# Seven block products for 13 channel pairs of two feed-forward passes

## The chip, the core and the metric

The kernel runs on one core of one Trainium2 chip. The core has five instruction streams that run side by side and wait for one another by semaphores: TensorE (PE, with its weight loads listed apart as PEld), VectorE (DVE), ScalarE (ACT), GpSimd (POOL) and SyncE (SP), which issues the DMAs. On-chip memory is SBUF and, for matmul results, PSUM. The metric is the device time of one execution in microseconds (us).

## The reference

Two residual layers work on 1024 tokens of 1024 channels. Layer 0 mixes tokens by gating and sparse attention, layer 1 by a convolution module, and each layer ends in the same feed-forward block, which the change is about:

```
x <- LayerNorm(alpha * x + f(x))
f:  u = x @ w_up                      # 1024 channels -> 2 x 2816
    u = causal 3-tap depthwise conv(u) + bias
    f(x) = (gelu(u[:, :2816]) * u[:, 2816:]) @ w_down
```

All operands and results are float32.

## The kernel before

**Numbers.** A float32 operand is cut into a high part, which TensorE reads in its float32r format, and the rest (`split`, `wload`): ACT copies the high part, and POOL or DVE subtracts it from the operand. A product is then three matmuls into the same PSUM tile, high x rest, rest x high, high x high (`mm3`, L77 to L79). Weights come as tiles of 128 x 1024 float32, 512 KB: the DMA L69, the copy `wh` on ACT (L70) and two subtractions `wl` of 128 x 512 on POOL (L73).

**Feed-forward.** The tokens are two halves of 512 (h = 0, 1), so there are four passes `ffn(h, l)`: F00, F10, F01, F11, in this order. In a pass, `up(j)` treats channel pair j of 22: for each of the two column tiles of the pair it loads a weight tile, makes 8 x 3 matmuls of 512 columns into the PSUM tile `pu`, and takes the three taps on ACT (L678, L680) and DVE (L682, L683, which copies the last two columns at L685). The first tile goes through gelu (L688); POOL multiplies it by the second (L690) and splits the result into `ph` and `pl`. `down(gi)` multiplies a group of pairs by the down weights: groups of 8, 8 and 6 pairs (`KG`), each in two halves of the output columns with four PSUM tiles `pd`. At the end of a half, four adds on DVE bring `pd` into the residual Z (L396 for the first group, L398 after it).

**Order.** The Python generators yield at the ends of units; `go` and `mix` interleave them, and the tile framework's scheduler orders each engine's instructions from that, so that products of two tiles interleave. An engine works strictly in its order. A tile name has a fixed number of buffers, and a new tile waits for the last reader of the old one. The normalisation of Z and its transposition (`norm`) is mixed into the neighbouring passes: `norm(1, g0)` runs at the start of F00, and the output norm `final(0, g3)` at the start of F11.

Of the kernel before, what the change touches and what calls it, by code (L numbers as in the profile page):

```python
# [37 lines left out]
def trunk_kernel(ctx, tc, xt, wab, wv, w280, wst, sgub, sgulg, sgulb, pe_k, pe_v, w1k, w1v, w2k, w2v,  # L38
# [613 lines left out]
    hal = fp.tile([128, 44, 2], F32, name="halo")  # L652
    cor = fp.tile([128, 44, 2], F32, name="cor")

    def ffn(h, l, tail=None):
        xh, xl = XT[h]
        z = Z[h]
        cw = V[f"fw{l}"].rearrange("p (m k) -> p m k", k=3)
# [8 lines left out]
                nc.vector.tensor_tensor(cor[:, :, i], cor[:, :, i], V[cb], op=OP.add)  # L667
        prod = {}

        def up(j):  # L670
            acc = []
            for e in range(2):
                mt = 2 * j + e
                w = wload(wup[l, mt])
# [2 lines left out]
                a = tmp("acc")
                nc.scalar.activation(a[:, 2 * h:], p[:, 2 * h:], AF.Identity, scale=cw[:, mt, 2:3], bias=col(cb, mt))  # L678
                for i in range(2 * h):
                    nc.scalar.activation(a[:, i:i + 1], p[:, i:i + 1], AF.Identity, scale=cw[:, mt, 2:3],  # L680
                                         bias=cor[:, mt, i:i + 1])
                nc.vector.scalar_tensor_tensor(a[:, 1:], p[:, :511], cw[:, mt, 1:2], a[:, 1:], op0=OP.mult, op1=OP.add)  # L682
                nc.vector.scalar_tensor_tensor(a[:, 2:], p[:, :510], cw[:, mt, 0:1], a[:, 2:], op0=OP.mult, op1=OP.add)  # L683
                if h == 0:
                    nc.vector.tensor_copy(hal[:, mt, :], p[:, 510:512])  # L685
                acc.append(a)
# [3 lines left out]
            nc.gpsimd.tensor_tensor(acc[0], acc[0], acc[1], op=OP.mult)  # L690
            hi = fp.tile([128, 512], F32R, name="ph", tag="p", bufs=18)
            lo = fp.tile([128, 512], F32R, name="pl", tag="p", bufs=18)
            split(hi, lo, acc[0], nc.gpsimd)
            prod[j] = (hi, lo)
# [288 lines left out]
```

## Time and profile before

| what | value |
|---|---|
| median of 3 runs | 2340.69 us (2338.47 to 2340.94) |
| the profiled execution | 2340.53 us |
| its span in the trace | 2338.8 us |
| PE busy | 2293.3 us, 98% |
| POOL, DVE, ACT busy | 1391.8, 1176.0, 1008.9 us |
| up matmuls `pu` of 512 columns | 4320 rows in the trace |
| down matmuls `pd` | 656 rows in each of three lines |

The span leaves 1.7 us of the execution outside. A matmul's end is modelled and a matmul overlaps the next, so its cost is the time from one start to the next, not the duration in the row. The share of an engine over the span hides how the stages differ; the rows below are of single stages.

### The profile page before, as it was taken

To read this page: it belongs to the slowest core of one execution; us is meant where nothing else is said; L and a number is where in the kernel's file an instruction comes from. 1 tells how busy PE (TensorE), PEld (TensorE's weight loads), DVE (VectorE), ACT (ScalarE), POOL (GpSimd) and SP (SyncE) were. 2 spreads that over 40 slices of the span, in tenths; PEclk is the share of its full clock that TensorE was granted. 3 is DMA by queue.
4 is the path that set the end of the run, shared out by engine and by line. 5 is a ranking of instruction groups with operands and counts; after the bars stand their busy time and mean duration, and the time that the engine had idled before them with its cause. 6 is when DMAs were issued, how large, how long until landed. Compare 5 with 4: busy or idle time off the path is not lost.

```text
span 2338.8 us, 30101 instructions
## 1 busy us (share of the span) xinstructions
PE 2293.3 (98%) x10959; PEld 1914.5 (82%) x10959; DVE 1176.0 (50%) x2176; ACT 1008.9 (43%) x1786; POOL 1391.8 (60%) x1313
## 2 busy tenths in 40 slices
PE   9999899999999999999999999999999999999998
PEld 7888789887888888788888887788888887888886
DVE  2532898746322223579972325589961446212214
ACT  4133998733433323434344552434243633534441
POOL 4442777556665656655566575655565666666672
PEclk9999999999999999999999999999999999999999
DMA  6153121352332333233323233223323233323340
GB/s 227 35 144 98 50 64 54 105 194 92 99 99 90 99 95 95 84 97 99 99 91 99 90 108 101 85 95 100 99 91 99 89 110 135 96 95 99 99 135 37
DMA packets 82988, 232.23 MB, mean 99 GB/s; under 512 B 10079, under 2 KB 24039, under 8 KB 82840
## 3 DMA queue, kind: packets, MB, share of 16 engines
q1 hardware_dynamic: 82840, 230.30, 31.2%
q8 instruction: 87, 1.43, 0.3%
q14 instruction: 61, 0.50, 0.1%
HBM read 213.44 MB, written 8.43 MB: 95 GB/s over the span
## 4 chain that ended last, share of the span: by engine, by line
PE 93%; DVE 3%; ACT 1%; issue 1%; POOL 1%; DMA 0%; SPq 0%; DVEq 0%; ACTq 0%
PE pu L77 13%; PE pu L79 13%; PE pu L78 13%; PE pd L77 9%; PE pd L78 9%; PE pd L79 9%; PE pt L563 2%; PE pca L79 1%; PE pcg L79 1%; PE pcg L77 1%; PE pca L77 1%; PE pcg L78 1%; PE pca L78 1%; PE O L571 1%; PE O L570 1%
## 5 line engine op out<-in xcount | busy, mean ns | idle before, releaser
L73 POOL TENSOR_TENSOR wl<-wraw,wh 128x512 fp32r<-128x512 f32 x680 | 889.1, 1330 | 704.7 <-ACT wh L70 693.7
L77 PE MATMUL pu<-XTl,wh 128*128 128x512 f32 x1440 | 564.7, 392 | 5.9 <-DVE acc L683 3.7
L79 PE MATMUL pu<-XTh,wh 128*128 128x512 f32 x1440 | 563.6, 391 | 0.0
L78 PE MATMUL pu<-XTh,wl 128*128 128x512 f32 x1440 | 563.0, 391 | 0.0
L70 ACT ACTIVATE wh<-wraw 128x1024 fp32r<-128x1024 f32 x340 | 359.6, 1058 | 414.3 <-PE pd L79 352.9
L682 DVE SCALAR_TENSOR_TENSOR acc<-pu,vec,acc 128x511 f32<-128x511 f32 x176 | 131.8, 749 | 513.0 <-ACT acc L680 264.6
L77 PEld LDWEIGHTS pu<-XTl,wh 128*128 128x128 f32 x1440 | 271.8, 189 | 62.8 <-issue 4.1
L758 DVE SCALAR_TENSOR_TENSOR cacc<-ht,vec,cacc 128x512 f32<-128x512 f32 x464 | 318.5, 751 | 5.5 <-ACT cacc L754 3.9
L678 ACT ACTIVATE acc<-pu,vec 128x510 f32<-128x510 f32 (+1 forms) x176 | 137.3, 780 | 424.0 <-PE pu L79 423.8
L79 PEld LDWEIGHTS pu<-XTh,wh 128*128 128x128 f32 x1440 | 271.5, 189 | 56.8
L78 PEld LDWEIGHTS pu<-XTh,wl 128*128 128x128 f32 x1440 | 271.7, 189 | 56.2
L77 PE MATMUL pd<-wl,ph 128*128 128x512 f32 x656 | 259.1, 396 | 0.0
L78 PE MATMUL pd<-wh,pl 128*128 128x512 f32 x656 | 258.8, 394 | 0.0
L79 PE MATMUL pd<-wh,ph 128*128 128x512 f32 x656 | 256.7, 395 | 0.0
L79 PEld LDWEIGHTS pd<-wh,ph 128*128 128x128 f32 x656 | 123.5, 188 | 29.0
L78 PEld LDWEIGHTS pd<-wh,pl 128*128 128x128 f32 x656 | 123.7, 189 | 28.6
L77 PEld LDWEIGHTS pd<-wl,ph 128*128 128x128 f32 x656 | 123.6, 188 | 28.4
L398 DVE TENSOR_TENSOR Z<-Z,pd 128x512 f32<-128x512 f32 x64 | 43.5, 683 | 180.1 <-PE pd L79 180.0
L683 DVE SCALAR_TENSOR_TENSOR acc<-pu,vec,acc 128x510 f32<-128x510 f32 x176 | 131.5, 747 | 4.7
L690 POOL TENSOR_TENSOR acc<-acc 128x512 f32<-128x512 f32 x88 | 113.7, 1292 | 25.0 <-DVE acc L683 17.6
L396 DVE SCALAR_TENSOR_TENSOR Z<-Z,pd 128x512 f32<-128x512 f32 x64 | 43.6, 682 | 156.6 <-PE pd L79 156.6
L540 POOL TENSOR_SCALAR P<-P,sm 128x64 f32<-128x64 f32 (+6 forms) x192 | 107.4, 583 | 21.9 <-DVE sm L534 12.8
(252 smaller groups left out, 3790.4 us busy)
## 6 DMA issues: line engine op xcount, KB each, us to landing
wraw<-wup SPq DMA_DIRECT2D x176, 512.0 KB, 3.5
wraw<-wdn SPq DMA_DIRECT2D x82, 512.0 KB, 3.5
wraw<-cwin SPq DMA_DIRECT2D x32, 512.0 KB, 3.5
wraw<-wout SPq DMA_DIRECT2D x16, 512.0 KB, 4.3
wraw<-cwout SPq DMA_DIRECT2D x16, 512.0 KB, 3.5
wraw<-wab SPq DMA_DIRECT2D x14, 512.0 KB, 3.9
gb<-lns SPq DMA_DIRECT2D x12, 512.0 KB, 4.2
B<-fd SPq DMA_DIRECT2D x8, 512.0 KB, 3.4
```

Of the source, the lines that this page charges most:

```text
L70: nc.scalar.activation(wh[:, :n], raw[:, :n], AF.Copy)
L73: (leng or nc.gpsimd).tensor_tensor(wl[:, c], raw[:, c], wh[:, c].bitcast(F32), op=OP.subtract)
L77: nc.tensor.matmul(out_, ah, bl, start=first, stop=False)
L78: nc.tensor.matmul(out_, al, bh, start=False, stop=False)
L79: nc.tensor.matmul(out_, ah, bh, start=False, stop=last)
L540: nc.gpsimd.tensor_scalar(P[:, e, o:o + ln_], P[:, e, o:o + ln_], sm[:, e, i:i + 1], 0.0, op0=OP.mult, op1=OP.add)
L563: nc.tensor.transpose(pt[:, j, e * 128:(e + 1) * 128], P[:, e, o:o + kn], ident)
L678: nc.scalar.activation(a[:, 2 * h:], p[:, 2 * h:], AF.Identity, scale=cw[:, mt, 2:3], bias=col(cb, mt))
L682: nc.vector.scalar_tensor_tensor(a[:, 1:], p[:, :511], cw[:, mt, 1:2], a[:, 1:], op0=OP.mult, op1=OP.add)
L683: nc.vector.scalar_tensor_tensor(a[:, 2:], p[:, :510], cw[:, mt, 0:1], a[:, 2:], op0=OP.mult, op1=OP.add)
L690: nc.gpsimd.tensor_tensor(acc[0], acc[0], acc[1], op=OP.mult)
L758: nc.vector.scalar_tensor_tensor(c[0] if k else ht[:, :H], ht[:, k:k + H], dww[:, j, k:k + 1], c[0], op0=OP.mult, op1=OP.add)
```

## The change

Only F00 and F11 (`quick=True`) are changed, and in them pairs 3 to 15, 13 of 22 (`QUICK`). For these a pair's product is a 2 x 2 block product (two weight tiles, two halves of the 1024 input channels, two halves of the 512 tokens), and it is made from seven block products instead of eight, by sums of blocks. Each block product (`prod7`) is 4 x 3 matmuls of 256 columns. What goes in and comes out:

- `sums`, once a pass: sums of the four token blocks, kept split in the tiles TA and TB (M2 to M7 below read them or blocks of x itself).
- `prep(j)`, once a pair: two weight tiles `ra`, `rb`; four adds of 128 x 512 on DVE for the sums s1 to s4 of weight blocks, `ws` the tile of two of them; splits of both tiles and of the four sums.
- `up7(j)`: the seven products into the PSUM tiles `pa` and `pb`, and between them a copy on ACT and five adds of 128 x 256 on DVE. The taps, gelu, gating (`taps3`, `gated`: the lines of `up`, moved) are the same.
- `downs`: pairs 0 to 15 go down in four groups of four, cut into 16 units of 24 matmuls; one unit follows each pair from j = 4 on. A group's adds into Z come with its second unit of each half. The last six pairs stay as they were.
- `norm(1, g0)` moves from the start of F00 to after its pair 15, and between the four `final(0, g3)` steps F11 goes one step instead of two. The scale and offset tiles are loaded a second time (`affine`).

```diff
-    def mm3(out_, ah, al, bh, bl, first, last):
+    def mm3(out_, ah, al, bh, bl, first, last, more=False):
...
+        def sums():
+            ta, tb = A("xh", F32R, (128, 4, 4, 256), name="TA"), A("xl", F32R, (128, 4, 4, 256), name="TB")
...
+            for k in (0, 2):
+                u1, u2 = (fp.tile([128, 2, 2, 256], F32, name="ts", tag="nrm", bufs=2) for _ in range(2))
...
+                nc.gpsimd.tensor_tensor(b11, *f(k, 0), op=OP.add)
+                nc.vector.tensor_tensor(b12, *f(k, 256), op=OP.add)
+                nc.gpsimd.tensor_tensor(b21, *f(k + 4, 0), op=OP.add)
+                nc.vector.tensor_tensor(b22, *f(k + 4, 256), op=OP.add)
+                nc.vector.tensor_tensor(b22, b22, b12, op=OP.subtract)
+                nc.vector.tensor_tensor(b12, b12, b11, op=OP.subtract)
+                nc.vector.tensor_tensor(b11, b22, b11, op=OP.add)
+                nc.vector.tensor_tensor(b21, b21, b11, op=OP.subtract)
+                for n, t_, e in (("t2", b11, nc.vector), ("t1", b12, nc.gpsimd), ("t3", b22, nc.vector),
+                                 ("t4", b21, nc.gpsimd)):
+                    split(X7[n][0][:, k:k + 2], X7[n][1][:, k:k + 2], t_, e)
...
+        def prep(j):
+            ra, rb = W4(F32, name="wraw"), W4(F32, name="wraw")
+            nc.sync.dma_start(ra, wup[l, 2 * j])
+            nc.sync.dma_start(rb, wup[l, 2 * j + 1])
+            s_ = fp.tile([128, 1024], F32, name="ws", tag="nrm", bufs=2)
+            a, b = slice(0, 512), slice(512, 1024)
+            add = lambda o, x_, y_, op: nc.vector.tensor_tensor(o, x_, y_, op=op)
...
+            def pair(src):
+                h_, l_ = W4(F32R, name="wh", tag="wh"), W4(F32R, name="wl", tag="wl")
+                nc.scalar.activation(h_, src, AF.Copy)
+                for c in (a, b):
+                    nc.gpsimd.tensor_tensor(l_[:, c], src[:, c], h_[:, c].bitcast(F32), op=OP.subtract)
...
+            def one(src, eng):
+                h_, l_ = (fp.tile([128, 512], F32R, name=n, tag="ht", bufs=8) for n in ("sh", "sl"))
+                split(h_, l_, src, eng)
+                return h_, l_
+            add(s_[:, a], rb[:, a], rb[:, b], OP.add)
+            add(s_[:, b], s_[:, a], ra[:, a], OP.subtract)
+            w["11"], w["12"] = pair(ra)
+            w["s2"] = one(s_[:, b], nc.vector)
+            w["s1"] = one(s_[:, a], nc.vector)
+            yield w
+            add(rb[:, a], ra[:, a], rb[:, a], OP.subtract)
+            add(ra[:, b], ra[:, b], s_[:, b], OP.subtract)
+            w["s3"], w["22"] = pair(rb)
+            w["s4"] = one(ra[:, b], nc.gpsimd)
+            yield
...
+        def prod7(o, w, x_, first=True):
+            for k in range(4):
+                s_ = slice(k * 128, (k + 1) * 128)
+                mm3(o, w[0][:, s_], w[1][:, s_], x_[0][:, k, :], x_[1][:, k, :], first and k == 0, k == 3, not first)
...
+        def up7(j):
...
+            prod7(pa[:, c0], w["11"], X7["11"])
+            prod7(pb[:, c1], w["s2"], X7["t2"])
+            nc.scalar.activation(t_, pa[:, c0], AF.Copy)
+            add(t_, t_, pb[:, c1])
+            prod7(pa[:, c0], w["12"], X7["21"], False)
+            nxt = prep(j + 1) if j + 1 < QUICK[1] else None
+            prod7(pa[:, c1], w["s1"], X7["t1"])
+            add(v_, t_, pa[:, c1])
+            if nxt:
+                W7[j + 1] = next(nxt)
+            yield
+            prod7(pb[:, c0], w["s3"], X7["t3"])
+            add(pb[:, c1], v_, pb[:, c0])
+            prod7(pa[:, c1], w["s4"], X7["22"], False)
+            add(pa[:, c1], t_, pa[:, c1])
+            acc = [taps3(2 * j, pa)]
+            nc.scalar.activation(acc[0], acc[0], AF.Gelu_apprx_tanh)
+            prod7(pb[:, c0], w["22"], X7["t4"], False)
+            if nxt:
+                next(nxt)
+            add(pb[:, c0], t_, pb[:, c0])
+            acc.append(taps3(2 * j + 1, pb))
+            gated(j, acc)
+            yield
...
+            def downs():
+                units = [(a, dh, i) for a in range(0, 16, 4) for dh in range(2) for i in range(2)]
...
-    F00 = ffn(0, 0)
-    mix(norm(1, g0), F00, 1)
-    go(F00, 56)
+    F00 = ffn(0, 0, quick=True)
+    go(F00, 2 * QUICK[1])
+    g0 = affine(0)
+    mix(norm(1, g0), F00, 2)
+    go(F00, 4)
...
-    F11 = ffn(1, 1, final(1, g3))
+    F11 = ffn(1, 1, lambda tt: final(1, g3)(tt), quick=True)
```

What the order of instructions becomes is shown at three places of F00. On POOL before, one pair of the up part alternates a weight tile (two `wl`) with one operation on the products (`acc` the gating, `pl` the split):

```order
L73 TENSOR_TENSOR wl_7189<-wraw_7187,wh_7188 128x512 [waits DMAHW4_49,PE_49,Activation_49]
L73 TENSOR_TENSOR wl_7189<-wraw_7187,wh_7188 128x512
L690 TENSOR_TENSOR acc_7055<-acc_7055,acc_7093 128x512 [waits DVE_49]
L73 TENSOR_TENSOR wl_7220<-wraw_7218,wh_7219 128x512 [waits DMAHW5_49,PE_49,Activation_49]
L73 TENSOR_TENSOR wl_7220<-wraw_7218,wh_7219 128x512
L63 TENSOR_TENSOR pl_7100<-acc_7055,ph_7099 128x512 [waits Activation_49]
```

After the change, this is one period of POOL, a pair with one down unit (L730 the subtractions of `prep` for `ra`, then for `rb`; L74 those of a down tile; L64 with `sl` the split of s4; L685 and L64 with `pl` the gating and its split):

```order
L64 TENSOR_TENSOR sl_8219<-wraw_8112,sh_8218 128x512 [waits PE_49,Activation_49]
L730 TENSOR_TENSOR wl_8214<-wraw_8113,wh_8213 128x512 [waits DMAHW1_49,Activation_49]
L730 TENSOR_TENSOR wl_8214<-wraw_8113,wh_8213 128x512
L685 TENSOR_TENSOR acc_8193<-acc_8193,acc_8223 128x512 [waits DVE_49,Activation_49]
L64 TENSOR_TENSOR pl_8230<-acc_8193,ph_8229 128x512 [waits Activation_49]
L730 TENSOR_TENSOR wl_8295<-wraw_8287,wh_8294 128x512 [waits DMAHW3_49,Activation_49]
L730 TENSOR_TENSOR wl_8295<-wraw_8287,wh_8294 128x512
L74 TENSOR_TENSOR wl_8337<-wraw_8335,wh_8336 128x512 [waits DMAHW5_49,Activation_49]
L74 TENSOR_TENSOR wl_8337<-wraw_8335,wh_8336 128x512
```

Two weight tiles and the two operations on the products were six instructions for a pair; a pair now has seven (with s4), and a down tile stands in each period, which makes nine. On DVE before, one pair is six instructions, none of which reads two tiles of SBUF without PSUM:

```order
L682 SCALAR_TENSOR_TENSOR acc_8383<-pu_8358,vec_233,acc_8383 128x511 [waits Activation_49,Pool_49]
L683 SCALAR_TENSOR_TENSOR acc_8383<-pu_8358,vec_233,acc_8383 128x510 [waits DVE_49]
L685 COPY halo_5749<-pu_8358 128x2
L682 SCALAR_TENSOR_TENSOR acc_8421<-pu_8396,vec_233,acc_8421 128x511 [waits Activation_49,Pool_49]
L683 SCALAR_TENSOR_TENSOR acc_8421<-pu_8396,vec_233,acc_8421 128x510 [waits DVE_49]
L685 COPY halo_5749<-pu_8396 128x2
```

After the change DVE has these rows in a period in which a down group ends (L723 the adds of `prep`, L766 those of `up7`, L400 the adds into Z, L64 the splits of s2 and s1; `wraw` is `ra` or `rb`):

```order
L723 TENSOR_TENSOR ws_8466<-wraw_8463 128x512 [waits DMAHW7_49]
L766 TENSOR_TENSOR tt_8410<-tt_8410,pb_8409 128x256 [waits PE_49,Activation_49]
L400 TENSOR_TENSOR Z_5526<-Z_5526,pd_8307 128x512 [waits PE_49]
L679 SCALAR_TENSOR_TENSOR acc_8398<-pb_8234,vec_233,acc_8398 128x510 [waits DVE_49]
L681 COPY halo_5749<-pb_8234 128x2
L723 TENSOR_TENSOR ws_8466<-ws_8466,wraw_8462 128x512 [waits DMAHW6_49,DVE_49]
L723 TENSOR_TENSOR wraw_8463<-wraw_8462,wraw_8463 128x512 [waits Pool_49]
L400 TENSOR_TENSOR Z_5526<-Z_5526,pd_8308 128x512 [waits PE_49]
L400 TENSOR_TENSOR Z_5526<-Z_5526,pd_8309 128x512 [waits PE_49]
L400 TENSOR_TENSOR Z_5526<-Z_5526,pd_8310 128x512 [waits PE_49]
L64 TENSOR_TENSOR sl_8475<-ws_8466,sh_8474 128x512 [waits Activation_49]
L64 TENSOR_TENSOR sl_8479<-ws_8466,sh_8478 128x512 [waits Activation_49]
```

The adds of the next pair's weights have moved among the taps and the adds into Z of this one, and the second of them (`ws` from `wraw`) stands behind an add into Z that waits for PE. On PE after the change, the products of this pair (`pa_7533`, `pb_7534`) interleave with the first ones of the next (`pa_7708`, `pb_7709`):

```order
L79 MATMUL pb_7534<-TB_6576,wh_7513 128x256 [waits DVE_49]
L80 MATMUL pb_7534<-TB_6576,wl_7514 128x256 [waits Pool_49]
...
L79 MATMUL pa_7708<-XTl_6020,wh_7594 128x256 [waits Activation_49]
L79 MATMUL pb_7709<-TA_6575,sh_7599 128x256 [waits DVE_49]
L80 MATMUL pb_7709<-TA_6575,sl_7600 128x256 [waits DVE_49]
...
L80 MATMUL pa_7708<-XTh_6019,wl_7595 128x256 [waits Pool_49]
...
L79 MATMUL pa_7533<-XTl_6020,sh_7518 128x256 [waits DVE_49]
L80 MATMUL pa_7533<-XTh_6019,sl_7519 128x256
```

The third product of sums (s4 in `sh_7518`) comes behind a wait for DVE, and so does the last one (`wh_7513` with TB); before, in the same place each tile of `pu` followed the other with waits for its weights alone.

## Rows read from the trace of the kernel before

**Rows 1.** The page's engine totals: busy us (share of the span) xinstructions.
```profile
PE 2293.3 (98%) x10959; PEld 1914.5 (82%) x10959; DVE 1176.0 (50%) x2176; ACT 1008.9 (43%) x1786; POOL 1391.8 (60%) x1313
```

**Rows 2.** Three stretches: busy us by engine, granted clock, DMA share, GB/s.
```profile
560.00:600.00 40.00, 37.11 (x171) 30.19 (x170) 29.16 (x44) 16.43 (x22) 25.70 (x19) 0.96 0.28 97
600.00:900.00 300.00, 300.00 (x1316) 246.79 (x1315) 71.72 (x132) 106.73 (x133) 186.21 (x148) 1.00 0.31 97
2010.00:2300.00 290.00, 290.00 (x1269) 238.18 (x1268) 63.47 (x86) 119.89 (x197) 189.08 (x145) 1.00 0.31 98
```

**Rows 3.** PE in F00, up matmuls: start us, duration us, instruction, shape.
```profile
644.73 0.39 PE L78 MATMUL pu<-XTh,wl 128*128 128x512 f32 x1
...
652.89 0.39 PE L78 MATMUL pu<-XTh,wl 128*128 128x512 f32 x1
```

**Rows 4.** PE in F00, matmuls of a down product.
```profile
699.81 0.40 PE L79 MATMUL pd<-wh,ph 128*128 128x512 f32 x1
...
716.78 0.40 PE L79 MATMUL pd<-wh,ph 128*128 128x512 f32 x1
```

**Rows 5.** PE early in the kernel, 256 columns, each with a new weight tile.
```profile
72.39 0.28 PE L78 MATMUL pg<-wsh,vl 128*128 128x256 f32 x1
...
73.69 0.40 PE L78 MATMUL pv<-wvh,XTl 128*128 128x512 f32 x1
```

**Rows 6.** The weight loads of the same stretch (PEld).
```profile
72.40 0.19 PEld L79 LDWEIGHTS pg<-wsh,vh 128*128 128x128 f32 x1
72.52 0.19 PEld L77 LDWEIGHTS pg<-wsl,vh 128*128 128x128 f32 x1
```

**Rows 7.** POOL in F00; in brackets the idle time before and what ended it.
```profile
647.18 2.55 POOL L73 TENSOR_TENSOR wl<-wraw,wh 128x512 fp32r<-128x512 f32 x2 [1.65 <-ACT wh L70]
649.69 1.29 POOL L63 TENSOR_TENSOR pl<-acc,ph 128x512 fp32r<-128x512 f32 x1
652.62 2.54 POOL L73 TENSOR_TENSOR wl<-wraw,wh 128x512 fp32r<-128x512 f32 x2 [1.65 <-ACT wh L70]
```

**Rows 8.** Groups of one form: xcount, busy us, mean ns, idle before and releasers.
```profile
L682 DVE SCALAR_TENSOR_TENSOR acc<-pu,vec,acc 128x511 f32<-128x511 f32 x176 | 131.8, 749 | 513.0 <-ACT acc L680 264.6 <-ACT acc L678 247.6
L63 DVE TENSOR_TENSOR ptl<-pt,pth 128x512 fp32r<-128x512 f32 x136 | 92.2, 686 | 28.2 <-ACT pth L62 21.7 <-PE pd L77 3.1 <-PE O L570 2.1
L63 DVE TENSOR_TENSOR ptl<-pt,pth 128x256 fp32r<-128x256 f32 x24 | 9.9, 414 | 0.2
L398 DVE TENSOR_TENSOR Z<-Z,pd 128x512 f32<-128x512 f32 x64 | 43.5, 683 | 180.1 <-PE pd L79 180.0
L70 ACT ACTIVATE wh<-wraw 128x1024 fp32r<-128x1024 f32 x340 | 359.6, 1058 | 414.3 <-PE pd L79 352.9 <-issue 36.1 <-DMA wraw<-wab 8.7
L62 ACT ACTIVATE ph<-acc 128x512 fp32r<-128x512 f32 x88 | 55.0, 625 | 49.7 <-POOL acc L690 49.7
```

**Rows 9.** The page's DMA issues: KB each, median us from issue to landing.
```profile
wraw<-wup SPq DMA_DIRECT2D x176, 512.0 KB, 3.5
```

**Rows 10.** POOL and DVE together, DVE with one operand in PSUM.
```profile
712.90 2.55 POOL L73 TENSOR_TENSOR wl<-wraw,wh 128x512 fp32r<-128x512 f32 x2 [3.04 <-ACT wh L70]
713.02 0.69 DVE L396 SCALAR_TENSOR_TENSOR Z<-Z,pd 128x512 f32<-128x512 f32 x1 [17.44 <-PE pd L79]
```

**Rows 11.** POOL and DVE together, DVE with both operands in SBUF, three places.
```profile
1054.38 2.96 POOL L73 TENSOR_TENSOR wl<-wraw,wh 128x512 fp32r<-128x512 f32 x2 [2.89 <-ACT wh L70]
1054.25 0.69 DVE L773 SCALAR_TENSOR_TENSOR ht<-th,ht 128x512 f32<-128x512 f32 x1
498.76 3.67 DVE L63 TENSOR_TENSOR mt<-mraw,mt 128x512 fp32r<-128x512 f32 x3 [0.17 <-ACT mt L62]
498.29 2.99 POOL L73 TENSOR_TENSOR wl<-wraw,wh 128x512 fp32r<-128x512 f32 x2 [3.33 <-ACT wh L70]
567.21 4.45 POOL L73 TENSOR_TENSOR wl<-wraw,wh 128x512 fp32r<-128x512 f32 x2 [0.99 <-ACT wh L70]
566.99 1.28 DVE L625 SCALAR_TENSOR_TENSOR Z<-Z,tm,gb 128x1024 f32<-128x1024 f32 x1
```

More of the change, by code (lines that the diff above doesn't have):

```diff
@@ L24 @@
 KG = [(0, 8), (8, 16), (16, 22)]
+QUICK = (3, 16)
 FW = 1152
@@ L74, in wload @@
         return wh, wl
-    def mm3(out_, ah, al, bh, bl, first, last):
-        nc.tensor.matmul(out_, ah, bl, start=first, stop=False)
-        nc.tensor.matmul(out_, al, bh, start=False, stop=False)
-        nc.tensor.matmul(out_, ah, bh, start=False, stop=last)
+    def mm3(out_, ah, al, bh, bl, first, last, more=False):
+        nc.tensor.matmul(out_, ah, bl, start=first, stop=False, skip_group_check=more)
+        nc.tensor.matmul(out_, al, bh, start=False, stop=False, skip_group_check=more)
+        nc.tensor.matmul(out_, ah, bh, start=False, stop=last, skip_group_check=more)
     def mtile(out_, w, xh, xl, kn=8):
@@ L668, in ffn, with taps3 @@
         prod = {}
+        def taps3(mt, p):
+            a = tmp("acc")
+            nc.scalar.activation(a[:, 2 * h:], p[:, 2 * h:], AF.Identity, scale=cw[:, mt, 2:3], bias=col(cb, mt))
+            for i in range(2 * h):
+                nc.scalar.activation(a[:, i:i + 1], p[:, i:i + 1], AF.Identity, scale=cw[:, mt, 2:3],
+                                     bias=cor[:, mt, i:i + 1])
+            nc.vector.scalar_tensor_tensor(a[:, 1:], p[:, :511], cw[:, mt, 1:2], a[:, 1:], op0=OP.mult, op1=OP.add)
+            nc.vector.scalar_tensor_tensor(a[:, 2:], p[:, :510], cw[:, mt, 0:1], a[:, 2:], op0=OP.mult, op1=OP.add)
+            if h == 0:
+                nc.vector.tensor_copy(hal[:, mt, :], p[:, 510:512])
+            return a
@@ L676, in up @@
                 mtile(p, w, xh, xl)
[L677 to L686, printed above, removed]
+                acc.append(taps3(mt, p))
                 if e == 0:
-                    nc.scalar.activation(a, a, AF.Gelu_apprx_tanh)
+                    nc.scalar.activation(acc[0], acc[0], AF.Gelu_apprx_tanh)
                     yield
[L690 to L694, printed above, removed]
+            gated(j, acc)
             yield
@@ L723, in down @@
                            into(h, gi == 0, gi == 2))
+        if quick:
+            src = lambda a, dh, i: wdn[l, (a + 2 * i) // 8 * 8 + dh * 4 + (a // 2 + i) % 4]
+            def downs():
+                units = [(a, dh, i) for a in range(0, 16, 4) for dh in range(2) for i in range(2)]
+                w = wload(src(*units[0]))
+                yield
+                for n, (a, dh, i) in enumerate(units):
+                    if i == 0:
+                        p = [psn("d", "pd") for _ in range(4)]
+                        done = into(h, a == 0, False)
+                    for tt in range(4):
+                        ts = slice(tt * 128, (tt + 1) * 128)
+                        for k in range(2):
+                            (ah, al), s_ = prod[a + 2 * i + k], slice(k * 512, k * 512 + 512)
+                            mm3(p[tt], ah[:, ts], al[:, ts], w[0][:, s_], w[1][:, s_], i == k == 0, i == k == 1)
+                        if i:
+                            done(tt, dh, p[tt])
+                    if n + 1 < len(units):
+                        w = wload(src(*units[n + 1]))
+                    yield
+            dn, sm = downs(), sums()
+            last = down_last(tail) if tail else None
+            for j in range(NPAIR):
+                if j == QUICK[0]:
+                    for _ in sm:
+                        pass
+                for i, _ in enumerate(up7(j) if QUICK[0] <= j < QUICK[1] else up(j)):
+                    if i == (j < 4) and j >= 3:
+                        next(dn, None)
+                    if QUICK[0] - 2 < j < QUICK[0]:
+                        next(sm, None)
+                    if tail and 16 <= j < 19:
+                        next(last)
+                    yield
+            yield from last if tail else product(lambda k: prod[16 + k], lambda dh, i: src(16, dh, i), 6,
+                                                 into(h, False, True))
+            return
         done = 0
@@ L878, in trunk_kernel @@
         final(0, g3)(tt)
-        go(F11, 2)
+        go(F11, 1)
+    go(F11, 2 * QUICK[1] - 4)
+    g3 = affine(3)
     go(F11)
```

28 lines of the change are left out of this document (27 added, 1 removed).

## The prediction

> **What bounds the kernel now.** I read the page's totals first: PE is busy 98% of the span, POOL, DVE and ACT 60, 50 and 43% [rows 1]. A mean can hide stages, so the second view is the busy time by stretch. The reader is to see that PE never idles in the steady part of both passes that change: 300.00 of 300 us in F00 and 290.00 of 290 in F11, at a granted clock of 1.00, with POOL at 62 and 65%, DVE at 24 and 22% [rows 2]. Only where the norm stands at the start of F00 does PE lose 40 − 37.11 = 2.9 us [rows 2]. So in these passes the time is the number of matmuls times their spacing, and the other engines have some 35% or more left. The third view is PE's order of time: the starts of 36 up matmuls span 652.89 − 644.73 = 8.16 us, 0.2267 each [rows 3]; 73 down matmuls take 16.97 us, 0.2325 each [rows 4].
>
> **PE's part of the change.** For each of 26 pairs (13 in two passes) 2 tiles × 8 × 3 = 48 matmuls of 512 columns become 7 × 4 × 3 = 84 of 256. The trace has such matmuls of 256 columns, each with a weight tile of its own: from the start of the first of eleven to the start of what follows them 1.30 us, 0.1182 each [rows 5]. 48 × 0.2267 = 10.88 us become 84 × 0.1182 = 9.93: 0.95 less per pair, 26 × 0.95 = **−24.8 us**. Half of 0.2267 would be the least (0.1134, −35 us); since rows 5 are the very shape I take them. From j = 4 on each pair has one down unit, 24 × 0.2325 = 5.58 us, so a period of PE was 16.46 us and becomes 15.51. The down matmuls themselves stay as many.
>
> **What the others must do in a period of 15.51 us.** POOL had for a pair six instructions of about 1.27 us (two back to back 2.54 or 2.55) [rows 7], and two more with a down tile; it now has nine in every period: ra, rb and a down tile with two each, the split of s4, the gating and its split. 9 × 1.27 = 11.4 us, 74%. DVE had, for a pair, four taps of 0.75 and two copies; it gets four adds and two splits of 128 x 512 at 0.69 and five adds of 256 at 0.41 [rows 8], 6.2 us, and four adds into Z of 0.68 in every second period: some 10.5 us on average. ACT gets three copies of 0.63 and one of 256. Each fits alone. What does not show in such sums is that POOL and DVE disturb each other. With one operand in PSUM a DVE operation leaves POOL at 2.55 us for two [rows 10]. With both in SBUF the two subtractions take 2.96 and 2.99, 0.42 to 0.45 more; three DVE subtractions take 3.67 us instead of 3 × 0.69, and beside the 1024-wide normalisation POOL needs 4.45 [rows 11]. All six new DVE operations of 512 on weights are of this kind, and before there was none in these periods. At 0.42 each they add 6 × 0.42 = 2.5 us to POOL's 11.4, at their full 0.69 4.1 us: 13.9 or 15.5 of 15.51. That is the tight resource after the change.
>
> The Trainium skill, SBUF — State Buffer, section "Who interferes with whom", says that a VectorE instruction with two SBUF inputs contends with a GpSimd instruction that reads SBUF, and that the one issued first holds the shared ports for its whole length. Rows 11 agree in kind; that the whole length counts is not what 0.42 shows. By the page the six would cost the full 4.1 us, the first rival below.
>
> **The loop that the new order makes.** POOL does the split of s4, which frees the buffer that the next pair's rb is loaded into: landing 3.5 us [rows 9]; then two adds on DVE (0.69 each), the copy of s2 (0.63) and of ra (1.06) on ACT, which works in order [rows 8], then on POOL ra's two (2.54), the down tile's two (2.54) and the next s4 split (1.27). 3.5 + 1.38 + 1.69 + 2.54 + 2.54 + 1.27 = 12.9 us: below 15.51. In every second period, where a down group ends, there stand in it as well, by the order of DVE and POOL, an add into Z behind PE (0.68), a tap (0.75), an add of 256 (0.41) and POOL's split of the product (1.29): 16.0 us, above PE. If the periods evened out (14.5 on average) PE would lose nothing; if not, half of them lose 0.5. PE's order puts products of s2 and s4 behind these, and all later matmuls queue behind a waiting one. With the disturbance once in each loop (0.42) they come to 13.3 and 16.5, and PE's periods to 15.51 and 16.5: a mean stall of 0.48 us. With all six at 0.42: 15.4 and 18.5, stall 1.5; at 0.69: up to 3. So the stall lies between 0 and 3 us for each of 24 periods (j = 4 to 15, twice). I take 0.48, the disturbance once, because four of the six can fall where POOL waits or where the loop has slack: **+11.5 us**. Nothing measured before shows how often they meet.
>
> **Starts and moves.** For pair 3 the sums and the weights have to be ready. `sums` is 8 operations on POOL (10.2 us) and 16 on DVE with both operands in SBUF (11 us); beside the usual work of POOL they are some 20 us of POOL and DVE excluding each other, and most of it can lie beside pairs 0 to 2 and what precedes them, where PE has over 30 us of matmuls. Between 0 (all covered) and 18 us (all in pair 2); I take 3 in F00. In F11 the sums meet the four output norms with their 1024-wide operations, +1.9 us on POOL for one such meeting [rows 11]: I take 4.5. Together **+7.5 us**. Moving norm(1) takes its gap of 2.9 us along; it can vanish or double at its new place: 0, ±2.9. The second loads of scale and offset, two of 512 KB, are covered by a DMA share of 0.31 [rows 2]: 0. The sixteen additional adds into Z of each pass are in DVE's sum and in the loop.
>
> **The sum.** −24.8 + 11.5 + 7.5 = −5.8 us. The profiled execution took 2340.53 us (span 2338.8 and 1.7 around it), 0.16 below the median of 2340.69: 2334.9 on the median's scale. A change of 0.2%, 4.7 us, is about what this measurement can tell from none: faster means below 2336.0, slower above 2345.4.
>
> **Rivals.**
> - *The ports and the buffer loop set the period* (slower). Each of six DVE operations meets POOL in the loop: the stall of 1.5 us on 24 periods is 37 us, and with −24.8 and +7.5 the time is 2360. It decides once the stall passes (24.8 − 7.5) / 24 = 0.72 us a period; above 0.92 the change is slower by over 0.2%. For it: the port's demand of 90 to 100% of the period, loads that can start only after a split, and DVE's adds of the next pair queued behind PE's down group. Against it: POOL is idle 35% now, and rows 11 show only part of a DVE operation's length lost. Chance 0.31. The whole lengths of which the Trainium skill speaks (SBUF — State Buffer, "Who interferes with whom") would make it the upper bound of 3 us a period, 2395.
> - *All is hidden*: the periods even out, no stall but 2 us at the starts: 2340.7 − 24.8 + 2 = 2318. For it: 12.9 us of loop and 74% of POOL, buffers that carry over one long period; against it: an add into Z that waits for PE in front of the next weights. Chance 0.17.
> - *The starts cost more*: 7.5 becomes 20 with the same steady stall: 2347. Chance 0.05.
> - *The change doesn't give what it says*: matmuls of 256 columns bound by their weight loads, 0.19 us each [rows 6]: 84 × 0.19 = 16.0 us a pair, +5.1, 26 times: +132 us, 2473. Against it: weight loads of 0.19 start 0.12 apart in the same rows, so they overlap. Chance 0.02.
>
> **How the numbers follow.** The forecast, a stall of 0.1 to 0.85 us a period, has 0.45 and its own range 2326 to 2344; about 0.27 of it lies below 2336.0 and 0.18 within 0.2%. With "all is hidden" faster has 0.44. Same is 0.18 and a part of the expensive starts, 0.20; slower is the loop, the rest of the starts and the weight loads, 0.36. The range starts at 2317, where nothing stalls, and reaches to 2364, a stall of some 1.7 us; beyond it lie the upper bounds of the stall and of the starts, some 0.15, and below it little more than 0.03.
>
> **What would show it.** In the profile after, block products should start 0.118 us apart where nothing waits, and PE's busy time in the window of pairs 4 to 15 should fall short by about 0.5 us in 15.5. The idle time should be put down to DVE adds or `sl` of the weight sums, or to POOL's `wl`, in periods with adds into Z. The mean of POOL's subtractions in these windows should rise above 1.29 us by some 0.1 to 0.3; if it stays, the ports are not the cause. A gap of some us each should stand at pair 3 of both passes, the larger one in F11. The forecast is wrong in its main step if PE loses nothing there, or above 0.9 us a period, and wrong in its first if the spacing is not 0.118.

## The result and the profile after

The changed kernel takes 2370.4 us (median of 4 runs, 2369.07 to 2372.07) against 2339.58 us before (4 runs): the ratio is 1.0132, interval 1.0114 to 1.015. It is 31 us slower, where 5.8 us faster was forecast, and outside the range that ended at 2364. Nearest is the first rival, the ports and the buffer loop, which was put at 2360: its ports were the cause, its buffer loop only a part of it (experiments 6 and 9).

First three windows of the changed kernel: busy us of PE, PEld, DVE, ACT and POOL with the count in brackets, then granted clock, DMA share, GB/s. The first and the last lie in the steady part of F00 and F11 and stand against [rows 2]; the middle one is the start of the block products in F11:

```profile
640.00:790.00 150.00, 139.72 (x948) 127.29 (x946) 113.98 (x169) 64.69 (x95) 111.36 (x80) 1.00 0.28 88
2017.00:2030.00 13.00, 7.19 (x39) 6.47 (x38) 12.46 (x14) 8.24 (x16) 9.20 (x7) 0.74 0.00 0
2060.00:2200.00 140.00, 136.24 (x915) 125.05 (x914) 103.73 (x142) 69.91 (x126) 105.24 (x75) 0.99 0.31 99
```

PE was busy for 300 of 300 us before [rows 2]; now it misses 10.3 of 150 in F00 and 3.8 of 140 in F11. Busy time also hides the part of a gap that a modelled matmul end covers. So the matmuls in the two windows were counted and each given its spacing: 0.118 us for 256 columns, 0.2325 for the down and 0.2267 for the up matmuls of 512. This work accounts for all but 14.2 and 7.5 us; before, the same sum leaves nothing in the same windows. Summed over both passes with their starts, 11 us were lost before and 68 after. So 57 us of waiting and low clock stand against a saving that came as forecast: the block products start 0.118 us apart where nothing waits, 26 pairs x (10.88 - 9.91) = 25 us. 57 - 25 = 32, against the 31 measured.

DVE in F00's steady window after, groups of one form (count, busy us, mean ns, idle before); the four adds of `prep`, its two splits, and the adds into Z as a measure:

```profile
L723 DVE TENSOR_TENSOR ws<-wraw 128x512 f32<-128x512 f32 x9 | 7.7, 851 | 18.7 <-DMA wraw<-wup 18.7
L723 DVE TENSOR_TENSOR ws<-ws,wraw 128x512 f32<-128x512 f32 x9 | 8.3, 921 | 0.2
L723 DVE TENSOR_TENSOR wraw<-wraw 128x512 f32<-128x512 f32 x9 | 11.7, 1297 | 0.0
L723 DVE TENSOR_TENSOR wraw<-wraw,ws 128x512 f32<-128x512 f32 x9 | 14.5, 1615 | 5.0 <-POOL wl L730 5.0
L64 DVE TENSOR_TENSOR sl<-ws,sh 128x512 fp32r<-128x512 f32 x18 | 22.1, 1248 | 2.6 <-ACT sh L63 2.3
L400 DVE TENSOR_TENSOR Z<-Z,pd 128x512 f32<-128x512 f32 x12 | 7.7, 676 | 0.0
```

The add into Z has one operand in PSUM and takes 0.68 us, as before [rows 8]. The six operations with both operands in SBUF need 0.85 to 1.62 us where 0.69 was charged: 7.2 us per pair instead of 4.1. POOL in the same window:

```profile
L730 POOL TENSOR_TENSOR wl<-wraw,wh 128x512 fp32r<-128x512 f32 x36 | 48.1, 1358 | 18.0 <-ACT wh L728 18.0
L74 POOL TENSOR_TENSOR wl<-wraw,wh 128x512 fp32r<-128x512 f32 x18 | 28.6, 1605 | 0.0
L685 POOL TENSOR_TENSOR acc<-acc 128x512 f32<-128x512 f32 x9 | 13.6, 1508 | 19.1 <-DVE halo L681 19.1
L64 POOL TENSOR_TENSOR pl<-acc,ph 128x512 fp32r<-128x512 f32 x9 | 13.8, 1529 | 3.0 <-ACT ph L63 3.0
```

The down tile's subtractions take 1.61 us, the product's split 1.53 and the gating 1.51, against 1.27 to 1.29 [rows 7]; the pair's own tiles take 1.36. Both engines' operations are longer beside each other's. How it reaches PE shows in a period in which a down group ends, DVE first (start us, duration us), then POOL and PE (idle time before and releaser in brackets):

```profile
745.14 0.69 DVE L723 TENSOR_TENSOR ws<-wraw 128x512 f32<-128x512 f32 x1 [2.37 <-DMA wraw<-wup]
746.08 0.68 DVE L400 TENSOR_TENSOR Z<-Z,pd 128x512 f32<-128x512 f32 x1
747.41 0.68 DVE L723 TENSOR_TENSOR ws<-ws,wraw 128x512 f32<-128x512 f32 x1
748.01 1.80 DVE L723 TENSOR_TENSOR wraw<-wraw 128x512 f32<-128x512 f32 x1
749.73 1.87 DVE L400 TENSOR_TENSOR Z<-Z,pd 128x512 f32<-128x512 f32 x3
751.52 1.33 DVE L64 TENSOR_TENSOR sl<-ws,sh 128x512 fp32r<-128x512 f32 x1
```

```profile
747.57 1.70 POOL L685 TENSOR_TENSOR acc<-acc 128x512 f32<-128x512 f32 x1 [3.62 <-DVE halo L681]
749.78 2.52 POOL L730 TENSOR_TENSOR wl<-wraw,wh 128x512 fp32r<-128x512 f32 x2 [0.52 <-ACT wh L728]
...
750.85 0.28 PE L79 MATMUL pb<-TA,sh 128*128 128x256 f32 x1
752.91 0.39 PE L80 MATMUL pb<-TA,sl 128*128 128x256 f32 x1 [1.78 <-DVE sl L64]
```

The add that makes s3 (`wraw<-wraw`) takes 1.80 us because POOL is in its gating at 747.57 to 749.27; the three adds into Z queue behind it, the split of s2 (1.33) behind these, and PE stands 1.78 us until that ends. The wait returns at 682.1, 716.3, 750.9 and 784.5 us, every second period, 17.1 us a period against 16.46 before. The waits of PE in that window (us in total, times, longest):

```profile
PE pb L80 <- DVE sl L64: 6.8, 4, 2.0
PE pb L79 <- DVE pb L766: 2.4, 4, 0.8
```

At the start in F11 the token sums meet POOL's weight work without a break. DVE, then POOL, then what PE waits for:

```profile
2014.42 1.60 DVE L709 TENSOR_TENSOR ts<-ts 128x512 f32<-128x512 f32 x1
2015.94 1.78 DVE L64 TENSOR_TENSOR TB<-ts,TB 128x512 fp32r<-128x512 f32 x1
2017.64 1.75 DVE L710 TENSOR_TENSOR ts<-ts 128x512 f32<-128x512 f32 x1
```

```profile
2013.73 3.44 POOL L730 TENSOR_TENSOR wl<-wraw,wh 128x512 fp32r<-128x512 f32 x2
2017.13 1.71 POOL L685 TENSOR_TENSOR acc<-acc 128x512 f32<-128x512 f32 x1
```

```profile
2017.31 0.39 PE L81 MATMUL pu<-XTh,wh 128*128 128x512 f32 x1
2023.13 0.55 PE L79 MATMUL pa<-XTl,wh 128*128 128x256 f32 x1 [5.44 <-DVE acc L679]
```

DVE takes 1.60 to 1.78 us for an operation, POOL 1.71 or 1.72 each: they alternate, and PE stands 5.44 us behind a tap that is queued among the sums. The DMA engines moved nothing in 2017 to 2030 us, and the mean granted clock there was 0.74.

In F00 the start is another case. The sums ran at 555.9 to 579.3 us, before the first block product, and PE waited 2.2 us among them. The longest wait there is for the first weight sum of pair 4, DVE's add first, then PE:

```profile
602.97 1.36 DVE L723 TENSOR_TENSOR ws<-wraw 128x512 f32<-128x512 f32 x1 [2.35 <-DMA wraw<-wup]
606.71 0.38 PE L79 MATMUL pb<-TA,sh 128*128 128x256 f32 x1 [3.70 <-ACT sh L63]
```

The load was issued at 599.71 us, when POOL's split of s4 of pair 3 had ended (599.69): here it is the buffer loop that holds PE.

### The profile page after: what moved, and what is told of

Read it like the earlier page. It is cut to its first block, busy times and chain, and to the rows that moved or that the text cites. A ratio compares the mean times of both kernels' runs of the same rounds, so it can differ in the third digit from the quotient of the medians.

```text
span 2368.4 us, 32680 instructions
## 1 busy us (share of the span) xinstructions
PE 2284.8 (96%) x11895; PEld 1947.5 (82%) x11895; DVE 1451.1 (61%) x2526; ACT 1064.2 (45%) x1906; POOL 1485.2 (63%) x1355
## 4 chain that ended last, share of the span: by engine, by line
PE 75%; DVE 9%; POOL 7%; issue 4%; DMA 3%; ACT 2%; DVEq 0%; SPq 0%; POOLq 0%; ACTq 0%
PE pu L79 9%; PE pu L80 9%; PE pu L81 9%; PE pd L79 8%; PE pd L81 8%; PE pd L80 8%; POOL wl L730 3%; DMA wraw<-wup 2%; POOL wl L74 2%; PE pt L565 2%; PE pca L79 1%; PE pcg L79 1%; PE pcg L80 1%; PE pca L80 1%; PE pcg L81 1%
## 5 line engine op out<-in xcount | busy, mean ns | idle before, releaser
L74 POOL TENSOR_TENSOR wl<-wraw,wh 128x512 fp32r<-128x512 f32 x576 | 769.7, 1359 | 534.0 <-ACT wh L71 522.9
L71 ACT ACTIVATE wh<-wraw 128x1024 fp32r<-128x1024 f32 x288 | 304.2, 1057 | 290.1 <-PE pd L81 238.3
L79 PE MATMUL pu<-XTl,wh 128*128 128x512 f32 x1024 | 402.4, 393 | 8.3 <-DVE acc L679 4.2
L81 PE MATMUL pu<-XTh,wh 128*128 128x512 f32 x1024 | 400.7, 391 | 0.0
L80 PE MATMUL pu<-XTh,wl 128*128 128x512 f32 x1024 | 400.3, 391 | 0.0
L678 DVE SCALAR_TENSOR_TENSOR acc<-pu,vec,acc 128x511 f32<-128x511 f32 x124 | 92.7, 747 | 277.0 <-ACT acc L676 139.1
L79 PEld LDWEIGHTS pu<-XTl,wh 128*128 128x128 f32 x1024 | 193.0, 188 | 49.7 <-issue 4.1
L81 PEld LDWEIGHTS pu<-XTh,wh 128*128 128x128 f32 x1024 | 193.1, 189 | 40.5
L80 PEld LDWEIGHTS pu<-XTh,wl 128*128 128x128 f32 x1024 | 193.2, 189 | 39.5
L674 ACT ACTIVATE acc<-pu,vec 128x512 f32<-128x512 f32 (+1 forms) x124 | 96.7, 779 | 275.0 <-PE pu L81 274.9
L730 POOL TENSOR_TENSOR wl<-wraw,wh 128x512 fp32r<-128x512 f32 x104 | 148.8, 1452 | 43.4 <-ACT wh L728 43.4
L685 POOL TENSOR_TENSOR acc<-acc 128x512 f32<-128x512 f32 x88 | 117.9, 1339 | 71.4 <-DVE acc L679 46.4
L400 DVE TENSOR_TENSOR Z<-Z,pd 128x512 f32<-128x512 f32 x96 | 64.0, 680 | 126.6 <-PE pd L81 126.5
L64 POOL TENSOR_TENSOR pl<-acc,ph 128x512 fp32r<-128x512 f32 x88 | 119.5, 1358 | 15.9 <-ACT ph L63 14.4
```

Of the source, the lines that this page charges most:

```text
L71: nc.scalar.activation(wh[:, :n], raw[:, :n], AF.Copy)
L79: nc.tensor.matmul(out_, ah, bl, start=first, stop=False, skip_group_check=more)
L80: nc.tensor.matmul(out_, al, bh, start=False, stop=False, skip_group_check=more)
L81: nc.tensor.matmul(out_, ah, bh, start=False, stop=last, skip_group_check=more)
L730: nc.gpsimd.tensor_tensor(l_[:, c], src[:, c], h_[:, c].bitcast(F32), op=OP.subtract)
```

## The experiments

Times are single runs beside a run of the kernel before on the same chip (2340.89 for experiments 1 to 4, 2338.38 for 5 to 8, 2339.45 for 9 to 11), except the last. The four runs of experiment 12 span 5.9 us, so a single run's step of 5 or 6 us is read with what the trace lost. "Lost" is PE's time in 640 to 790 and 2060 to 2200 us beyond its matmuls' spacings, as above: after 14.2 and 7.5.

**1. The down groups without block products.**

```diff
-                for i, _ in enumerate(up7(j) if QUICK[0] <= j < QUICK[1] else up(j)):
+                for i, _ in enumerate(up(j)):
```

> Block products taken out: pairs 3 to 15 of F00 and F11 are made by the old up (48 matmuls of 512 columns), without sums and weight sums; the down groups of four, the moved norm(1) and the moved steps of final(0) stay as in the change. Theory A (the loss of 31 us sits in what the block products bring with them: weight sums, their loop and the starts): about the time of the kernel before, 2340 +- 4. Rival R (the regrouped down product, its 32 additional adds into Z and the moved norm cost a good part): 2348 or more.

2342.53 us, 1.6 above the run beside it: without the block products the regrouping, the 32 additional adds into Z and the moved norm cost next to nothing. Theory A holds.

**2. One input in SBUF.**

```diff
-            add = lambda o, x_, y_, op: nc.vector.tensor_tensor(o, x_, y_, op=op)
...
+                    nc.vector.tensor_reduce(o, x_.rearrange("p (n o) -> p n o", o=1), axis=mybir.AxisListType.X, op=OP.add)
+            add = lambda o, x_, y_, op: one_in(o, x_)
...
-                split(h_, l_, src, eng)
+                if eng is nc.vector:
+                    nc.scalar.activation(h_, src, AF.Copy)
+                    one_in(l_, h_.bitcast(F32))
+                else:
+                    split(h_, l_, src, eng)
```

`one_in` is the reduction; the split of s4 stays on POOL as it was, and with it the buffer loop.

> The six DVE operations on weights of each pair (four adds, the subtractions of the splits of s2 and s1) become single-input reductions over one element with the same output shape, so the weight sums and two low parts are left out of the result; DVE's instruction count and order in the loop stay. Theory P (the steady stall, some 27 us of lost PE time between pair 4 and 15 of both passes, comes from DVE and POOL excluding each other when DVE has two operands in SBUF): the steady stall falls to under 8, POOL's mean of the weight subtractions falls from 1.45 to about 1.30 us, time 2350 +- 4. Theory Q (DVE's queue: adds into Z stand in front of the splits that PE waits for) and theory B (loads start too late because ra's buffer is held to the split of s4): 2364 to 2370.

2337.37 us, 33 less than the changed kernel, below even what theory P said. DVE and POOL in F00's steady window, and the two windows:

```profile
L726 DVE TENSOR_REDUCE wraw<-wraw 128x512 f32<-128x512 f32 x19 | 12.9, 680 | 5.7 <-POOL wl L734 5.7
L726 DVE TENSOR_REDUCE sl<-sh 128x512 fp32r<-128x512 f32 x18 | 12.0, 678 | 3.9 <-ACT sh L740 3.5
L74 POOL TENSOR_TENSOR wl<-wraw,wh 128x512 fp32r<-128x512 f32 x20 | 26.5, 1349 | 0.0
```

```profile
640.00:790.00 150.00, 149.96 (x1052) 139.69 (x1051) 97.38 (x180) 70.36 (x102) 111.60 (x87) 1.00 0.33 106
2060.00:2200.00 140.00, 140.00 (x983) 130.50 (x982) 87.98 (x153) 75.58 (x135) 102.70 (x81) 1.00 0.33 110
```

The same number of DVE operations takes 0.68 us each, POOL's down tile is at 1.35 instead of 1.61, and nothing is lost (the two sums come out at -0.2 and -0.6, the accuracy of the method). But with the second operands the run also drops waits between the operations; experiment 9 keeps the second operands.

**3. Adds into Z behind the splits.**

```diff
                         if i:
-                            done(tt, dh, p[tt])
+                            with tc.issue_after(LS[0]):
+                                done(tt, dh, p[tt])
```

`LS[0]` is the split of s1.

> The adds into Z of a down group are queued on DVE behind the split of s1 of the next pair; nothing else changes. Theory Q: PE's waits for sl (8.8 us in F00 and 5.5 in F11 in the steady part) nearly go, and what follows them: 2354 +- 4. Theory P: DVE is late by its meetings with POOL, the adds into Z only add 1.9 of some 5 us per two periods: 2364 to 2370. Theory B: 2366 to 2371.

2372.32 us: nothing gained. In F00's window the wait for `sl` is gone from PE's list, and others have its place:

```profile
PE pa L80 <- POOL wl L730: 2.8, 6, 1.0
PE pb L79 <- DVE pb L769: 2.3, 5, 0.8
```

Lost: 10.2 and 8.6. Theory Q falls: the adds into Z were in front of PE's split, but they were not what made DVE late.

**4. Two splits moved from POOL to DVE.**

```diff
-            split(hi, lo, acc[0], nc.gpsimd)
+            split(hi, lo, acc[0], nc.vector if quick and QUICK[0] <= j < QUICK[1] else nc.gpsimd)
...
-            w["s4"] = one(ra[:, b], nc.gpsimd)
+            w["s4"] = one(ra[:, b], nc.vector)
```

> In the 26 pairs the split of s4 and the split of the gated product move from POOL (1.27 us each) to DVE (0.69 each, both operands in SBUF). Theory P: POOL's and DVE's excluding times sum to 1.2 us less per period, 2360 +- 4. Theory Q: two more operations in DVE's queue, 2373 or more. Theory B: s4's buffer is free about 0.6 us earlier, 2366 +- 3.

2392.86 us, 22 slower; theory P in this form was wrong, and theory Q's 2373 or more came true. DVE in F00's steady window, and the windows:

```profile
L64 DVE TENSOR_TENSOR pl<-acc,ph 128x512 fp32r<-128x512 f32 x9 | 12.0, 1335 | 0.7 <-ACT ph L63 0.3
L723 DVE TENSOR_TENSOR wraw<-wraw,ws 128x512 f32<-128x512 f32 x8 | 13.1, 1638 | 4.2 <-POOL wl L730 4.2
```

```profile
640.00:790.00 150.00, 139.13 (x930) 125.25 (x929) 118.83 (x182) 64.36 (x93) 88.54 (x59) 1.00 0.26 88
2060.00:2200.00 140.00, 130.80 (x863) 118.31 (x862) 104.86 (x145) 65.26 (x116) 81.48 (x55) 0.99 0.26 88
```

POOL fell from 111 to 89 us busy in 150, DVE rose from 114 to 119, and the moved split takes 1.34 us instead of 0.69. So the sum of the two engines' excluding times is not what decides. An operation with two SBUF operands on DVE came out up to 1.1 us longer beside one of POOL (1.80 instead of 0.68), and all that is queued on DVE waits with it, the taps and the adds that PE needs; two more of them there made it worse.

**5. Other starts.**

```diff
-                    if QUICK[0] - 2 < j < QUICK[0]:
+                    if i == 0 and j in (0, 1):
                         next(sm, None)
+                    if first:
+                        if i == 0:
+                            W7[j + 1] = next(first)
+                        else:
+                            next(first)
...
+    go(F11, 2 * 16)
+    g3 = affine(3)
     for tt in range(4):
         final(0, g3)(tt)
         go(F11, 1)
```

`first` is `prep(3)`, beside pair 2.

> Only the order of the starts changes: the two halves of the token sums are issued beside pairs 0 and 1 (not beside pair 2), the weights of pair 3 beside pair 2, and in F11 all four steps of final(0) come after pair 15. Theory S (the waits up to pair 4, 11 us in F00 and 22 us in F11 with the low clock that follows them, come from what is piled onto DVE and POOL there): F11's start falls to that of F00, 2355 +- 5. Rival (the work excludes itself wherever it stands, so the waits only move): 2366 to 2372.

2365.8 us. PE's waits and low clock from 50 us before the first block product of F11 to 25 us after fell from 21.8 to 7.8 us, but the stretch behind it, to the last block product, lost 12 more: the rival was nearer. About 6 of the 12 stand in the last 45 us, where the four output norms now run; the others are in the periods before. What the start saved was paid behind it.

**6. ra's buffer freed earlier.**

```diff
-            add(ra[:, b], ra[:, b], s_[:, b], OP.subtract)
+            add(s_[:, b], ra[:, b], s_[:, b], OP.subtract)
...
-            w["s4"] = one(ra[:, b], nc.gpsimd)
+            w["s4"] = one(s_[:, b], nc.gpsimd)
```

> The weight sum s4 is written into the tile ws instead of over ra, so ra's buffer is free after one DVE add instead of after POOL's split of s4, some 2 to 3 us earlier; nothing else changes. Theory B (the loop is limited by the buffer that the next load waits for): 2358 +- 4. Theory P (limited by DVE and POOL excluding each other): 2365 to 2371.

2364.1 us, 6 less: between the two. Lost 8.7 and 8.8, and 8.4 us instead of 12.0 from 50 us before the first block product of F00 to 25 us after. The buffer loop of the prediction has a part, in F00 alone, and not the main one.

**7 and 8. Fewer pairs.** The starts of 5 and the tile of 6, with

```diff
-                for i, _ in enumerate(up7(j) if QUICK[0] <= j < QUICK[1] else up(j)):
+                for i, _ in enumerate(up7(j) if j in QSET else up(j)):
+QSET = (3, 4, 6, 7, 9, 10, 12, 13, 15)      # run 7
+QSET = (3, 5, 7, 9, 11, 13, 15)             # run 8
```

> Block products for nine of the 13 pairs only (two of three: 3, 4, 6, 7, 9, 10, 12, 13, 15), the others by the old up; starts as in the run with the changed starts and s4 in ws. Theory P: an old pair has 16.5 us and no DVE operation with two SBUF operands, which gives the loop slack; PE gains 18 x 0.95 = 17 us, starts cost some 15, steady stalls under 8: 2345 +- 6. Theory Q: the adds into Z hold the splits as before: 2355 or more.

> Block products for every other pair (3, 5, ... 15: seven in a pass), otherwise as the run with two of three. Theory P: no steady stall, PE gains 14 x 0.95 = 13 us, starts cost some 12: 2340 +- 5, below the run with two of three or level with it. Theory Q: still a stall of about 2 us in each period with adds into Z: 2350 or more.

2350.44 and 2349.01 us: run 7 within what P said, run 8 above it by 4. In run 8 PE's list has no wait for `sl`, but one for the copy of the first block product on ACT, 4.8 us in F00 and 9.8 in F11, probably because a single block pair between old ones has no neighbour's products to fill that time; no run tests this. Both stay 10 us and more above the kernel before.

**9. The weight sums in PSUM.**

```diff
-            s_ = fp.tile([128, 1024], F32, name="ws", tag="nrm", bufs=2)
+            sa, sb = psn("u", "wsa"), psn("c", "wsb")
...
-            add(s_[:, a], rb[:, a], rb[:, b], OP.add)
-            add(s_[:, b], s_[:, a], ra[:, a], OP.subtract)
+            add(sa, rb[:, a], rb[:, b], OP.add)
+            add(sb, sa, ra[:, a], OP.subtract)
...
-            add(rb[:, a], ra[:, a], rb[:, a], OP.subtract)
-            add(ra[:, b], ra[:, b], s_[:, b], OP.subtract)
+            s4 = fp.tile([128, 1024], F32, name="ws", tag="nrm", bufs=2)[:, a]
+            add(rb[:, a], rb[:, b], sb, OP.subtract)
+            add(s4, ra[:, b], sb, OP.subtract)
```

> The whole computation is kept, but the sums s1 and s2 of the weight blocks lie in two PSUM tiles (one each from the buffers of pa and pb), s3 is made as A22 - s2, and s4 goes into an SBUF tile of its own: five of the six DVE operations on weights have one operand in PSUM, one keeps two in SBUF. Theory P: the lengthening of DVE and POOL goes as in the run with single-input operations, the steady stall falls under 10 us, the starts stay: 2345 +- 6. Rival (the single-input run won by the dependencies it dropped, the wait for ra and for ACT's copies, not by the ports; and pa and pb now share their buffers with the sums): 2362 or more.

2341.44 us, 29 less, with the whole computation kept. DVE and POOL in F00's steady window, and the windows:

```profile
L723 DVE TENSOR_TENSOR wsa<-wraw 128x512 f32<-128x512 f32 x9 | 14.0, 1553 | 5.0 <-DMA wraw<-wup 5.0
L723 DVE TENSOR_TENSOR wsb<-wsa,wraw 128x512 f32<-128x512 f32 x9 | 6.2, 694 | 0.2
L723 DVE TENSOR_TENSOR wraw<-wraw,wsb 128x512 f32<-128x512 f32 x10 | 6.7, 675 | 0.0
L74 POOL TENSOR_TENSOR wl<-wraw,wh 128x512 fp32r<-128x512 f32 x20 | 27.4, 1391 | 0.0
```

```profile
640.00:790.00 150.00, 149.85 (x1057) 139.76 (x1056) 104.54 (x183) 70.51 (x105) 112.16 (x87) 1.00 0.31 103
2060.00:2200.00 140.00, 140.00 (x976) 130.19 (x975) 90.97 (x153) 75.27 (x137) 107.75 (x82) 1.00 0.33 109
```

The one operation that still reads two SBUF tiles (`wsa`) takes 1.55 us, all others 0.68 to 0.69. Lost: 0.5 and 0.2 us. The edit also puts s4 into a tile of its own, as experiment 6 does; that alone left 8.7 and 8.8 us lost, so the rest is the operands' place. Experiment 2, which kept the buffer loop and lost nothing, says the same from the other side. Together they settle the steady part; the split of the 29 us between the two edits is not exact.

**10 to 12. The starts again, and the token sums.** Run 10 is 9 with the starts of 5; in run 11 two of the four token sums of each half lie in PSUM as well, so that three of eight DVE operations read two SBUF tiles; run 12 is run 11 again, with more than one execution.

```diff
-                b11, b12, b22, b21 = u1[:, 0], u1[:, 1], u2[:, 0], u2[:, 1]
...
+                b11, b21, b12 = u1[:, 0], u1[:, 1], u2[:, 0]
+                b22, n11 = (psn("d", "ps", (128, 2, 256)) for _ in range(2))
...
-                nc.vector.tensor_tensor(b11, b22, b11, op=OP.add)
-                nc.vector.tensor_tensor(b21, b21, b11, op=OP.subtract)
+                nc.vector.tensor_tensor(n11, b22, b11, op=OP.add)
+                nc.vector.tensor_tensor(b21, b21, n11, op=OP.subtract)
```

> As the run with the sums in PSUM, and the starts ordered as in the run with the changed starts. Theory P and S together: once the steady part has room, what is taken from the starts stays taken: 2334 +- 6, below the kernel before. Rival: as before the work only moves, 2343 or more.

> As the run before it, and in the token sums five of eight DVE operations of each half get an operand in PSUM (two of the tiles there). Theory P: 11 us of DVE work that excludes POOL becomes 4, another 2 to 5 us at the starts: 2331 +- 6. Rival (the starts are limited by DVE's amount of work and PSUM tiles taken from the down products): level with the run before it or slower.

> The kernel of the run before (weight sums and two of the token sums in PSUM, changed starts) again, timed in three rounds against the kernel before. If the ports are the cause and nothing but chance lies between two runs of one kernel, 2324 +- 3 again, a ratio to before of 0.993 with an interval that leaves out 1.

2330.51, 2323.66, and for run 12 2328.3 us (median of 4 runs, 2325.96 to 2331.82) against 2340.6: ratio 0.9948, interval 0.9928 to 0.9969. Run 11 came out below what was expected, run 12 above it. This version is faster than both kernels; than the one before by 0.5%. The windows of run 12:

```profile
640.00:790.00 150.00, 149.86 (x1052) 139.54 (x1052) 103.44 (x182) 68.95 (x103) 113.71 (x87) 1.00 0.31 103
2060.00:2200.00 140.00, 137.19 (x941) 126.76 (x940) 99.49 (x155) 70.11 (x124) 107.69 (x79) 1.00 0.35 117
```

Nothing is lost in F00's (0.6 us); 3.7 us in F11's, whose window takes in the end of the block products. Now the changed starts pay more (11 us from 9 to 10, 4.6 in 5). Two runs of one kernel lay 4.6 us apart here, from 11 to 12, so steps of that size are not told apart, and what the token sums in PSUM are worth stays open.

## Why the prediction was wrong

**PE's gain** was right: 24.8 us forecast, 25 found, at the spacing of [rows 5].

**The step that failed** is "with the disturbance once in each loop (0.42)". The 0.42 us is what POOL lost in [rows 11]; what DVE lost was in the same rows (three subtractions in 3.67 us instead of 2.07) and was not charged, though DVE is the engine whose queue PE waits for. The price of 0.69 came from [rows 8], where `pt` is a matmul result in PSUM; with both operands in SBUF it held where POOL was idle (0.69 at 745.14 us above), but not in the mean. Measured, the six operations cost DVE 3.1 us a period more, and the down tile and the product's split cost POOL about 0.9, with the gating and the pair's own tiles 1.5. "Four of the six can fall where POOL waits or where the loop has slack" was wrong: POOL is busy for 111 of 150 us, and the order puts them beside its operations. The stall was 1.6 us a period in F00 (14.2 us in 8.8 periods) and 0.9 in F11, some 30 us for 24 periods, instead of 0.48 and 11.5. By the prediction's own sign, above 0.9 us a period, its main step was wrong in F00; its other sign came as said, the mean of POOL's subtractions for weight tiles (L730 and L74 above) rose from 1.29 to 1.44 us.

The first rival, with a chance of 0.31, had the ports right and a stall of 1.5, near F00's 1.6 and above F11's 0.9. But it charged them to POOL and the buffer loop, at 0.42 us each; the runs show them in DVE's queue. That its 2360 comes near 2370 is in part luck.

The Trainium skill, SBUF — State Buffer, section "Who interferes with whom", says that whichever instruction was issued first keeps the shared ports to its end and the other blocks. On DVE's side the trace agrees, 1.80 us for an operation of 0.68 beside POOL's; on POOL's side the loss of 1.71 - 1.27 = 0.44 us is less than DVE's 0.68.

**The starts** cost about 28 us more than before, not 7.5. In F11 [rows 11] were read as 1.9 us for one meeting, and what the alternation of DVE and POOL through 20 us of sums does to the taps was not worked out; in F00, where the sums were covered but for 2.2 us, the buffer loop of the first pairs was not counted. This account is read from the traces; experiments 5 and 10 show only that the order of the starts moves it. A part of it is the clock: after PE's long waits matmuls are spaced at 0.21 us for a while. Here is PE before and after a wait of 3.58 us in F00, where the granted clock falls from the 2.4 to the 1.2 GHz level, then the window around it with its mean granted clock of 0.79:

```profile
813.46 0.28 PE L81 MATMUL pb<-TB,wh 128*128 128x256 f32 x1
813.57 0.28 PE L79 MATMUL pb<-TB,wh 128*128 128x256 f32 x1
...
820.00 0.58 PE L79 MATMUL pa<-XTl,wh 128*128 128x256 f32 x1 [3.58 <-ACT tt L769]
820.59 0.41 PE L81 MATMUL pa<-XTh,wh 128*128 128x256 f32 x1
820.80 0.41 PE L79 MATMUL pa<-XTl,wh 128*128 128x256 f32 x1
```

```profile
816.00:824.00 8.00, 4.42 (x23) 4.00 (x22) 8.00 (x11) 3.15 (x4) 7.53 (x6) 0.79 0.27 95
```

Summed over all matmuls that are spaced so, this is 15 us in the two passes, against 3 before.

**The buffer loop** was in the sum with the right parts, at undisturbed lengths; experiment 6 shows that it was not the main limit. **Nothing for the moved norm** was about right: its gap at the new place is the one of the last rows, some 5 us with the clock, as at the old.

## What to carry to other kernels

Before work goes to an idle DVE beside a busy POOL, look at where its operands lie: with one of them in PSUM it cost 0.68 us here, with both in SBUF 0.85 to 1.62 on average and up to 1.8, and every instruction behind it in the queue was late by as much. Price such a meeting on both engines, by the one that the bottleneck waits for, and don't add up two engines' busy times as if one could fill the other's gaps. A saving at a start can be paid again behind it: the same change of order was worth 4.6 us here while the steady part was over its limit, and 11 once it had room, both from single runs.

## What the runs showed of the hardware

- DVE and POOL, both with two SBUF operands, alternate when neither pauses: 1.60 to 1.78 us for a DVE operation of 0.68, 1.71 for one of POOL of 1.27.
- A reduction over one element (one SBUF operand) takes 0.68 us on DVE for 128 x 512 and leaves POOL nearly alone: its down tile was at 1.35 us.
- Matmuls of 256 columns with a new weight tile each hold 0.118 us over whole windows, and 84 weight loads in place of 48 did not show beyond that here.
